# mLSTM denominators summed on GpSimd with one product by ones per head, and position-bias tiles laid out by the host

## The chip, the cores and the metric

The kernel runs on one core of one Trainium2 chip. The metric is the device time of one execution in microseconds (us), lower is better. The engines are TensorE (PE, with its weight loads shown as PEld), VectorE (DVE), ScalarE (ACT), GpSimd (POOL) and SyncE (SP, which here only issues DMAs). Each engine works through its own queue in order.

## What is computed

One decoder layer on a sequence of 512 tokens and 1024 features: RMSNorm, one wide projection, two parallel token mixers (an mLSTM with 4 heads of 128, and differential attention with 4 heads), a gated merge, a gated convolutional FFN, a per-layer embedding and a final norm. The parts that the change touches are these lines, cut from the reference:

```python
# mLSTM, a head: weights of keys for queries, numerator and denominator
sqk = jnp.einsum('bhcld,bhcsd->bhcls', qc, kc) * dmat
num = (...
       + jnp.einsum('bhcls,bhcse->bhcle', sqk, vc))
den = s_inter * ... + jnp.sum(sqk, -1)
h = num / jnp.maximum(jnp.abs(den), jnp.exp(-m_t))[..., None]
# differential attention: scores of a half of a head
bucket = t5_causal_bucket(q_pos, k_pos)
bias = jnp.moveaxis(rel_bias[bucket], -1, 0)
...
s = jnp.einsum('bhqd,bhkd->bhqk', qb, kk, ...) * scale + bias
```

The kernel evaluates the mLSTM not in chunks of 64 but over the whole sequence at once, which is the same sum; so `den` of a head is the column sum, over all 512 keys, of a matrix of weights that is zero where the key comes after the query.

## The kernel before, in words

Activations lie with features on the 128 partitions and the 512 tokens along the free dimension. Every product is made of three passes (`mm3`, lines 96 to 99): each operand is split into a high part and a low part (`split`, line 87: a copy on ACT, a subtraction on DVE), and high x high, high x low and low x high are accumulated in PSUM. Weights come in chunks of 128 x 1024 (`wload`, line 101), each loaded by SP, cast by ACT (L89) and completed by DVE (L90), with two buffers each for `raw`, `whi` and `wlo`.

The program is a Python trace; a planner then orders each engine's queue when the program is built, by program order as priority and by its own estimates of time, and hands out buffers by tag. Nothing is reordered on the chip. The string `ORDER` gives the order of the steps of both branches: `bias0` and `if0` (gates) come first, then projections `mq`, `mk` with convolution, the cores `m0` to `m3` of the mLSTM heads and their ends `M0` to `M3`, then attention (`dq`, `dk`, `dv`, cores `a`, ends `A`), with the merge gates `ga`, `gb` as work in between.

A core `m` (function `mlstm`) runs over four blocks of 128 keys, j = 0 to 3. For each it loads a row of gate terms to all partitions (`rb`, SP, L419; widths 512, 384, 256, 128), takes the exponential (ACT, L420), clears the upper triangle of the diagonal block (POOL, L421), multiplies by the scores `s` from PSUM (DVE, L425) and splits the result into `ph` and `pl`. `weighted` (L381) then multiplies them by V into `num` (three passes) and by a matrix of ones into `den` (two passes, L394 and L395). The PSUM widths are 512, 384, 256 and 256 columns; the last block is padded with zeros by POOL. `den` has every row equal to the column sum. The tag `rb` has three buffers, `hn` four, the PSUM tag `acc` two.

`mlstm_end` reads `den` (L442), forms a correction for the norm and normalises `num`; its norm uses `colsum` (L157): copy on ACT (L159), subtraction on DVE (L160), two products with ones (L161, L162).

`gates` (`if0`) makes the gate pre-activations from one projection, and runs a chain of small DVE and ACT operations: products (L302, L303), sums (L306), logarithm of the sigmoid (L309 to L313), a running maximum (L317), four running sums (L322). The columns that ACT needs as biases are transposed on PE into `colp` (L331).

`make_bias` (`bias0`) makes the attention's Toeplitz tiles on the chip: a table, two one-hot matrices by DMA, two full-precision products on PE (`bvp`, L347), a copy scaled by 8 on ACT, a row in DRAM, a broadcast of it to 128 rows in DRAM, and four skewed loads of 256 KB from there, all of these DMAs on POOL's queue. `make_nlam` loads the lambda vectors and reduces them on DVE. In `attention` a DVE instruction (L467) adds scores and bias with the scale 0.125 and takes the maximum.

Of the kernel before, what the change touches and what calls it, by code (L numbers as in the profile page):

```python
# [20 lines left out]
H = 4  # L21
# [11 lines left out]
# columns of the packed per-feature parameters  # L33
# [8 lines left out]
# offsets of a head's broadcast gate rows: one run for each block of keys, then -m  # L42
# [3 lines left out]
# chunks that ScalarE scales for the final norm; the last ones are scaled as they are normed  # L46
NSCALED = 6

# the steps of the two branches, by priority: projections, then the cores (m, a) and their ends (M, A)
ORDER = """  # L50
bias0 if0 mq0 mk0 mq1 mk1 m0 m1 mk3 mq2 dk0 M0 M1 mk2 m2 mq3 M2 m3 dq0 dv0 M3 a0 dk1 dq1
# [5 lines left out]
def trunk_kernel(ctx, tc, xT, pT, par, oneh, relb, lamv, w_if, w_in, w_v, w_br, w_out, w_up,  # L57
# [88 lines left out]
    def rsqrt_of(r, v, a, before=None):  # L146
        """r = v ** -0.5: from its logarithm, then one Newton step; a is scratch."""
# [44 lines left out]
    def win(c):  # L192
        return wload(w_in[c])

    def conv_silu(c, scale, name):
# [3 lines left out]
        nc.gpsimd.memset(u[:, 0:3], 0.0)  # L199
# [13 lines left out]
    def halves(c, name):  # L213
        """a head's two halves of 64 features, each in its own rows."""
        o = ps("mm", name)
        proj(o, win(c), 0, h)
        y = tt("ev", "y")
        nc.vector.tensor_mul(y, o, rB)
        return y, (slice(0, 64), slice(64, P))

    def queries(c, name):
        """for each half, one operand with its two parts above one another."""
        y, rows = halves(c, name)
# [8 lines left out]
    def keys(c, name):  # L232
        """for each half, its first part twice, and its second part beside zeros."""
# [12 lines left out]
    def vw(i, g, kk, old):  # L246
        """a half at a time, so that the first products can start early."""
# [42 lines left out]
    def gates():  # L290
        # few columns: the second parts of the weights stand beside the first ones
# [45 lines left out]
    def make_bias():  # L337
        tab = cp.tile([REL_BUCKETS + 1, H], F32, name="tab")
        nc.vector.memset(tab, NEG)
        nc.gpsimd.dma_start(tab[0:REL_BUCKETS, :], relb)  # L340
        bvd = dp.tile([H, 640], F32, name="bvd")
        for i in range(2):
            half = slice(i * 320, (i + 1) * 320)
            oh = tt("hn", "oh", 320)[0:REL_BUCKETS + 1, :]
            nc.gpsimd.dma_start(oh, oneh[:, half])
            o = ps("acc", "bvp", 320)
            nc.tensor.matmul(o[0:H, :], lhsT=tab, rhs=oh, start=True, stop=True)  # L347
            bv = tt("hn", "bv", 320)[0:H, :]
            nc.scalar.activation(bv, o[0:H, :], AF.Copy, scale=8.0)
            nc.gpsimd.dma_start(bvd[:, half], bv)  # L350
        rows = dp.tile([P, H * 640], F32, name="bvrows")
        nc.gpsimd.dma_start(rows, bvd.rearrange("h u -> (h u)").partition_broadcast(P))
        bias = []
        for hh in range(H):
            t = f(rt("bt", f"bias{hh}"))
            src = bass.AP(tensor=rows.tensor, offset=rows[0, hh * 640 + P - 1:hh * 640 + P].offset,
                          ap=[[H * 640 - 1, P], [1, S]])
            nc.gpsimd.dma_start(t, src)
            bias.append(t)
        return bias  # L360
# [17 lines left out]
    def wide(j):  # L378
        """columns of a block of keys: of all the later queries, 256 at the least."""
        return min(j * P, S - 2 * P)  # L380

    def weighted(name, j, src_parts, v, hh, outs):
        """products with V (and with ones) of one block of keys; src_parts fills the block's pair."""
# [6 lines left out]
        o = outs[0][:, wide(j):]  # L390
        mm3(o, [t[:, hh * P:(hh + 1) * P] for t in v[j]], (ph, pl), j == 0, j == NB - 1)
        if len(outs) > 1:
            o = outs[1][:, wide(j):]
            nc.tensor.matmul(o, lhsT=ones, rhs=ph, start=j == 0, stop=False)  # L394
            nc.tensor.matmul(o, lhsT=ones, rhs=pl, start=False, stop=j == NB - 1)  # L395

    def head_norm(o, g, name, extra=None):
        """y = o * g * rsqrt(mean square of o over a head's 128 features + extra)."""
# [15 lines left out]
    def mlstm(hh):  # L414
        num, den = ps("acc", f"num{hh}"), ps("acc", f"den{hh}")
        for j in range(NB):
# [9 lines left out]
            weighted("p", j, lambda a, b: split(a, b, rb), mv, hh, (num, den))  # L426
# [27 lines left out]
    def attention(hh, q, k):  # L454
        av = []
        for i in range(NB):
# [3 lines left out]
            for z in range(2):  # L460
                s = ps("sc", f"ds{hh}{i}{z}", nw)
                for b in range(2):
# [5 lines left out]
                    out=e, in0=s[:, :n], in1=bias[hh][:, S - n:], scale=0.125, scalar=-3.0e38,  # L468
# [10 lines left out]
        for j in range(NB):  # L479
# [3 lines left out]
            weighted("a", j, lambda a, b: split(a, b, tps), dv, hh, (o,))  # L483
# [213 lines left out]
def _fmajor(a):  # L697
    """(S, K*128) -> (128, K, S)."""
    return a.T.reshape(a.shape[1] // P, P, a.shape[0]).transpose(1, 0, 2)
# [70 lines left out]
```

## Time and profile before

| what | value |
|---|---|
| three runs | 835.82, 835.96, 836.72 us (median 835.96) |
| profiled execution: span from first to last instruction | 833.1 us |
| median less that span | 2.9 us |
| PE busy | 809.5 us of the span (97%) |
| DVE, ACT, POOL busy | 552.0, 423.5, 25.0 us |
| mean granted TensorE clock, as a share of full speed | 0.991 |

The profile gives one execution's span and no separate time for what lies around it; the runs' median is 2.9 us above it. Matmul durations in the trace overlap, since matmuls are pipelined; what one costs the engine is read from the start of one to the start of the next. "Idle before" is the time for which the engine had nothing running ahead of an instruction, with what ended it.

### The profile page before, as it was taken

To read this page: it belongs to the slowest core of one execution; us is meant where nothing else is said; L and a number is where in the kernel's file an instruction comes from. 1 tells how busy PE (TensorE), PEld (TensorE's weight loads), DVE (VectorE), ACT (ScalarE), POOL (GpSimd) and SP (SyncE) were. 2 spreads that over 40 slices of the span, in tenths; PEclk is the share of its full clock that TensorE was granted. 3 is DMA by queue.
4 is the path that set the end of the run, shared out by engine and by line. 5 is a ranking of instruction groups with operands and counts; after the bars stand their busy time and mean duration, and the time that the engine had idled before them with its cause. 6 is when DMAs were issued, how large, how long until landed. Compare 5 with 4: busy or idle time off the path is not lost.

```text
span 833.1 us, 9821 instructions
## 1 busy us (share of the span) xinstructions
PE 809.5 (97%) x3626; PEld 662.6 (80%) x3626; DVE 552.0 (66%) x877; ACT 423.5 (51%) x627; POOL 25.0 (3%) x110
## 2 busy tenths in 40 slices
PE   6999999999999999999999999999999999999993
PEld 5778788887878888888788888888888888888883
DVE  6588888699767854456677777777777333343676
ACT  6546887687776433234654444444445332222653
POOL 0111100000000000000000000000000000000000
PEclk9999999999999999999999999999999999999997
DMA  6263323221222223352333322223322333333212
GB/s 222 92 207 111 116 97 123 89 77 62 66 76 76 76 102 101 122 182 95 107 102 101 101 95 87 98 101 101 101 89 89 94 96 111 90 95 95 100 53 101
DMA packets 29143, 85.42 MB, mean 103 GB/s; under 512 B 3286, under 2 KB 7018, under 8 KB 28968
## 3 DMA queue, kind: packets, MB, share of 16 engines
q1 hardware_dynamic: 28424, 82.22, 30.5%
q0 software_dynamic: 672, 2.59, 1.0%
q8 instruction: 28, 0.46, 0.2%
q14 instruction: 19, 0.16, 0.1%
HBM read 82.66 MB, written 3.45 MB: 103 GB/s over the span
## 4 chain that ended last, share of the span: by engine, by line
PE 90%; DVE 3%; ACT 2%; DMA 2%; issue 1%; SPq 0%; DVEq 0%; ACTq 0%
PE wd L99 5%; PE uv L97 5%; PE wd L97 5%; PE uv L99 5%; PE uv L98 5%; PE wd L98 5%; PE ug L97 5%; PE ug L99 5%; PE ug L98 5%; PE ga L97 2%; PE ga L99 2%; PE ga L98 2%; PE wo L97 2%; PE gb L97 2%; PE gb L98 2%; PE gb L99 2%
## 5 line engine op out<-in xcount | busy, mean ns | idle before, releaser
L89 ACT CAST whi<-raw 128x1024 fp32r<-128x1024 f32 (+1 forms) x143 | 144.5, 1012 | 214.3 <-PE wd L98 71.2
L90 DVE TENSOR_TENSOR wlo<-raw,whi 128x1024 fp32r<-128x1024 f32 (+1 forms) x142 | 167.1, 1178 | 90.0 <-ACT whi L89 88.7
L97 PE MATMUL wd<-gh,whi 128*128 128x512 f32 x176 | 68.5, 389 | 0.0
L98 PE MATMUL wd<-gl,whi 128*128 128x512 f32 x176 | 68.5, 389 | 0.0
L99 PE MATMUL wd<-gh,wlo 128*128 128x512 f32 x176 | 68.5, 389 | 0.0
L576 DVE SCALAR_TENSOR_TENSOR y<-u,prm,y 128x512 f32<-128x512 f32 x88 | 65.6, 748 | 1.5
L89 ACT CAST gh<-y 128x512 fp32r<-128x512 f32 x22 | 13.7, 621 | 55.5 <-DVE y L585 55.5
L571 DVE TENSOR_TENSOR u<-uv,rffn 128x512 f32<-128x512 f32 x22 | 15.2, 692 | 38.1 <-PE uv L99 38.1
L98 PEld LDWEIGHTS wd<-gl,whi 128*128 128x128 f32 x176 | 33.0, 188 | 6.9
L99 PEld LDWEIGHTS wd<-gh,wlo 128*128 128x128 f32 x176 | 33.0, 188 | 6.9
L97 PEld LDWEIGHTS wd<-gh,whi 128*128 128x128 f32 x176 | 33.0, 188 | 6.8
L574 ACT ACTIVATE y<-u,prm 128x512 f32<-128x512 f32 x44 | 35.7, 814 | 0.5 <-DVE u L571 0.3
L583 ACT ACTIVATE y<-y 128x512 f32<-128x512 f32 x22 | 13.9, 632 | 40.6 <-DVE y L576 40.6
L90 DVE TENSOR_TENSOR gl<-y,gh 128x512 fp32r<-128x512 f32 x22 | 15.2, 692 | 14.7 <-ACT gh L89 14.7
L97 PE MATMUL wo<-mxh,whi 128*128 128x512 f32 x64 | 24.9, 389 | 0.0
L98 PE MATMUL wo<-mxl,whi 128*128 128x512 f32 x64 | 24.9, 389 | 0.0
L99 PE MATMUL wo<-mxh,wlo 128*128 128x512 f32 x64 | 24.9, 389 | 0.0
L143 ACT ACTIVATE sq<-x 128x512 f32<-128x512 f32 x27 | 16.7, 620 | 9.3 <-DVE x L633 9.3
L471 ACT ACTIVATE e<-e,mx 128x128 f32<-128x128 f32 (+3 forms) x32 | 17.8, 558 | 7.0 <-DVE mx L470 6.8
L144 DVE TENSOR_TENSOR acc<-acc,sq 128x512 f32<-128x512 f32 x27 | 18.5, 686 | 3.1 <-ACT sq L143 3.0
L205 DVE SCALAR_TENSOR_TENSOR y<-u,prm,y 128x512 f32<-128x512 f32 x24 | 17.9, 745 | 2.0 <-ACT y L203 1.9
L559 DVE TENSOR_TENSOR x<-x,wo 128x512 f32<-128x512 f32 x8 | 5.5, 688 | 17.1 <-PE wo L99 17.1
(1060 smaller groups left out, 2206.1 us busy)
## 6 DMA issues: line engine op xcount, KB each, us to landing
raw<-in_w_up SPq DMA_DIRECT2D x44, 512.0 KB, 3.2
raw<-in_w_in SPq DMA_DIRECT2D x36, 512.0 KB, 3.3
raw<-in_w_down SPq DMA_DIRECT2D x16, 512.0 KB, 3.5
x<-in_xT SPq DMA_DIRECT2D x16, 256.0 KB, 4.4
raw<-in_w_br SPq DMA_DIRECT2D x8, 512.0 KB, 3.2
raw<-in_w_out SPq DMA_DIRECT2D x8, 512.0 KB, 3.7
raw<-in_w_gate SPq DMA_DIRECT2D x8, 512.0 KB, 3.2
raw<-in_w_down SPq DMA_DIRECT2D x8, 384.0 KB, 3.1
```

The costliest lines, as they stand in the source:

```text
L89: nc.scalar.copy(hi, src)
L90: nc.vector.tensor_sub(lo, src, f(hi))
L97: nc.tensor.matmul(o, lhsT=lh, rhs=rh, start=start, stop=False)
L98: nc.tensor.matmul(o, lhsT=lh, rhs=rl, start=False, stop=False)
L99: nc.tensor.matmul(o, lhsT=ll, rhs=rh, start=False, stop=stop)
L143: nc.scalar.activation(q, src, AF.Square)
L144: nc.vector.tensor_add(acc, acc, q)
L205: nc.vector.scalar_tensor_tensor(y, u[:, i:i + S], col(c0 + i), y, op0=ALU.mult, op1=ALU.add)
L471: nc.scalar.activation(e, e, AF.Exp, bias=mx[:, 1:2], accum_out=mx[:, 2:3])
L571: nc.vector.tensor_mul(u[:, 2:514], o, rB)
L574: nc.scalar.activation(y, u[:, 2:514], AF.Identity, scale=col(c0 + 2), bias=col(c0 + 3))
L576: nc.vector.scalar_tensor_tensor(y, u[:, i:i + S], col(c0 + i), y, op0=ALU.mult, op1=ALU.add)
```

## The change

Four things change.

1. `weighted` no longer multiplies the blocks by ones. Instead `mlstm` keeps the tile `rb` of block 0 as `total`, adds the tiles of blocks 1 to 3 to its columns on GpSimd, and makes one `colsum` of it into `den`.
2. `make_bias` only loads four finished tiles of 256 KB from an input `biasT`, which the host lays out (`_bias_tiles`). The step `bias0` moves from the front of `ORDER` to behind `mk2`; the loads, still on POOL's queue, are issued after the last small memset that POOL did for a convolution. `make_nlam` moves with the step.
3. The scale 1/8 moves from the attention's DVE instruction (its `scale` is now 1.0) to the queries' scaling by the norm, which becomes a `scalar_tensor_tensor` instead of a `tensor_mul`; the factor 8 on the bias goes.
4. Comments and docstrings go; they change nothing.

```diff
-bias0 if0 mq0 mk0 mq1 mk1 m0 m1 mk3 mq2 dk0 M0 M1 mk2 m2 mq3 M2 m3 dq0 dv0 M3 a0 dk1 dq1
+if0 mq0 mk0 mq1 mk1 m0 m1 mk3 mq2 dk0 M0 M1 mk2 bias0 m2 mq3 M2 m3 dq0 dv0 M3 a0 dk1 dq1
...
-        nc.gpsimd.memset(u[:, 0:3], 0.0)
+        nonlocal last_pool
+        last_pool = nc.gpsimd.memset(u[:, 0:3], 0.0)
...
-    def halves(c, name):
+    def halves(c, name, scale=1.0):
...
-        nc.vector.tensor_mul(y, o, rB)
+        nc.vector.scalar_tensor_tensor(y, o, scale, rB, op0=ALU.mult, op1=ALU.mult)
...
     def make_bias():
-        tab = cp.tile([REL_BUCKETS + 1, H], F32, name="tab")
...
-            nc.tensor.matmul(o[0:H, :], lhsT=tab, rhs=oh, start=True, stop=True)
...
+        out = []
         for hh in range(H):
             t = f(rt("bt", f"bias{hh}"))
-            src = bass.AP(tensor=rows.tensor, offset=rows[0, hh * 640 + P - 1:hh * 640 + P].offset,
-                          ap=[[H * 640 - 1, P], [1, S]])
-            nc.gpsimd.dma_start(t, src)
-            bias.append(t)
-        return bias
+            with tc.issue_after(last_pool.ins):
+                nc.gpsimd.dma_start(t, biasT[:, hh * S:(hh + 1) * S])
+            out.append(t)
+        return out
...
-    def weighted(name, j, src_parts, v, hh, outs):
+    def weighted(name, j, src_parts, v, hh, o):
...
-        o = outs[0][:, wide(j):]
-        mm3(o, [t[:, hh * P:(hh + 1) * P] for t in v[j]], (ph, pl), j == 0, j == NB - 1)
-        if len(outs) > 1:
-            o = outs[1][:, wide(j):]
-            nc.tensor.matmul(o, lhsT=ones, rhs=ph, start=j == 0, stop=False)
-            nc.tensor.matmul(o, lhsT=ones, rhs=pl, start=False, stop=j == NB - 1)
+        mm3(o[:, wide(j):], [t[:, hh * P:(hh + 1) * P] for t in v[j]], (ph, pl), j == 0, j == NB - 1)
...
-            weighted("p", j, lambda a, b: split(a, b, rb), mv, hh, (num, den))
+            weighted("p", j, lambda a, b: split(a, b, rb), mv, hh, num)
+            if j == 0:
+                total = rb
+            else:
+                nc.gpsimd.tensor_add(total[:, j * P:], total[:, j * P:], rb)
+        colsum(den, total)
         return num, den
...
-                    out=e, in0=s[:, :n], in1=bias[hh][:, S - n:], scale=0.125, scalar=-3.0e38,
+                    out=e, in0=s[:, :n], in1=bias[hh][:, S - n:], scale=1.0, scalar=-3.0e38,
```

## Rows read from the trace of the kernel before

**Rows 1.** The page, part 1: busy us (share of the span) xinstructions.
```profile
PE 809.5 (97%) x3626; PEld 662.6 (80%) x3626; DVE 552.0 (66%) x877; ACT 423.5 (51%) x627; POOL 25.0 (3%) x110
```

**Rows 2.** Windows by stage, the mLSTM's: length, busy us (xinstructions), PEclk, DMA share, GB/s.
```profile
65.00:155.00 90.00, 88.95 (x421) 73.37 (x421) 74.13 (x116) 69.93 (x113) 9.17 (x31) 1.00 0.32 106
```

**Rows 3.** Waits of PE: what waited for whom: us in total, times, longest.
```profile
PE colp L331 <- DVE cols L323: 1.6, 1, 1.6
PE num L97 <- ACT pph L89: 1.0, 3, 0.4
```

**Rows 4.** Timeline of PE, head 1: start us, us, line, out<-in, shape.
```profile
87.75 0.39 PE L99 MATMUL num<-pph,mvl 128*128 128x512 f32 x1
87.98 0.40 PE L395 MATMUL den<-ppl,ones 128*128 128x512 f32 x1
...
88.74 0.33 PE L394 MATMUL den<-pph,ones 128*128 128x384 f32 x1
88.92 0.33 PE L395 MATMUL den<-ppl,ones 128*128 128x384 f32 x1
89.09 0.28 PE L97 MATMUL num<-pph,mvh 128*128 128x256 f32 x1
89.21 0.28 PE L394 MATMUL den<-pph,ones 128*128 128x256 f32 x1
```

**Rows 5.** Timeline of PE around the first product of the position bias.
```profile
32.77 0.39 PE L99 MATMUL mvp<-whi,h7l 128*128 128x512 f32 x1
...
33.09 0.70 PE L347 MATMUL bvp<-oh,tab 33*4 33x320 f32 x2
...
33.72 0.50 PE L300 MATMUL if<-h0h,whi 128*128 128x512 f32 x1
```

**Rows 6.** Timeline of PE around a column sum of today's head norm.
```profile
109.38 0.50 PE L161 MATMUL hm1ss<-csph,ones 128*128 128x512 f32 x1
...
109.72 0.39 PE L98 MATMUL mk<-h7l,whi 128*128 128x512 f32 x1
...
110.18 0.42 PE L162 MATMUL hm1ss<-cspl,ones 128*128 128x512 f32 x1
...
110.44 0.40 PE L97 MATMUL mq<-h0h,whi 128*128 128x512 f32 x1
```

**Rows 7.** Groups of ACT and of DVE, 60 to 160 us: xcount, busy us, mean ns.
```profile
L159 ACT CAST csph<-v 128x512 fp32r<-128x512 f32 x4 | 2.5, 620 | 0.1
...
L160 DVE TENSOR_TENSOR cspl<-v,csph 128x512 fp32r<-128x512 f32 x4 | 2.8, 690 | 1.7 <-ACT csph L159 1.7
```

**Rows 8.** Groups of POOL: xcount, busy us, mean ns, idle before.
```profile
L421 POOL TENSOR_SCALAR_AFFINE_SELECT rb<-rb 128x128 f32<-128x128 f32 x16 | 5.8, 361 | 48.7 <-ACT rb L420 40.7 <-DVE ppl L90 5.7 <-issue 2.4
```

**Rows 9.** Timeline of DVE and POOL side by side, from 81.65 us.
```profile
81.65 1.23 DVE L90 TENSOR_TENSOR wlo<-raw,whi 128x1024 fp32r<-128x1024 f32 x1 [0.24 <-ACT whi L89]
...
82.77 0.85 POOL L421 TENSOR_SCALAR_AFFINE_SELECT rb<-rb 128x128 f32<-128x128 f32 x1 [2.39 <-issue]
82.79 0.69 DVE L93 SCALAR_TENSOR_TENSOR mk1l<-y,mk1h 128x512 fp32r<-128x512 f32 x1
```

**Rows 10.** Timeline of PE around its wait for the gate columns.
```profile
50.34 0.39 PE L99 MATMUL mq<-h1h,wlo 128*128 128x512 f32 x1
...
52.31 0.22 PE L331 MATMUL colp<-ident,cols 4*128 4x4 f32 x1 [1.58 <-DVE cols L323]
...
57.03 0.39 PE L99 MATMUL mq<-h5h,wlo 128*128 128x512 f32 x1
```

**Rows 11.** Window behind that wait, columns as in rows 2.
```profile
52.40:57.00 4.60, 4.60 (x13) 3.49 (x14) 4.60 (x11) 0.63 (x1) 0.00 (x0) 0.63 0.60 212
```

**Rows 12.** Timeline of DVE, start of the gate chain.
```profile
37.68 0.68 DVE L302 TENSOR_TENSOR gt<-if,rmix 36x512 f32<-36x512 f32 x1 [1.52 <-PE if L300]
...
40.21 0.69 DVE L303 TENSOR_TENSOR g<-if,rmix 36x512 f32<-36x512 f32 x1
```

**Rows 13.** Waits of SP's own queue, columns as in rows 3.
```profile
SPq L419 <- DVE ppl L90: 17.8, 8, 4.0
```

More of the change, by code (lines that the diff above doesn't have):

```diff
@@ L56, in trunk_kernel @@
 @with_exitstack
-def trunk_kernel(ctx, tc, xT, pT, par, oneh, relb, lamv, w_if, w_in, w_v, w_br, w_out, w_up,
+def trunk_kernel(ctx, tc, xT, pT, par, biasT, lamv, w_if, w_in, w_v, w_br, w_out, w_up,
                  w_down, w_gate, w_ple, out):
@@ L193, in win @@
         return wload(w_in[c])
+    last_pool = None
     def conv_silu(c, scale, name):
@@ L217, in halves @@
         y = tt("ev", "y")
-        nc.vector.tensor_mul(y, o, rB)
+        nc.vector.scalar_tensor_tensor(y, o, scale, rB, op0=ALU.mult, op1=ALU.mult)
         return y, (slice(0, 64), slice(64, P))
     def queries(c, name):
-        y, rows = halves(c, name)
+        y, rows = halves(c, name, 0.125)
         qs = []
@@ L337, in make_bias @@
     def make_bias():
-        tab = cp.tile([REL_BUCKETS + 1, H], F32, name="tab")
[L339 to L346, printed above, removed]
-            nc.tensor.matmul(o[0:H, :], lhsT=tab, rhs=oh, start=True, stop=True)
[L348 to L353, printed above, removed]
+        out = []
         for hh in range(H):
             t = f(rt("bt", f"bias{hh}"))
-            src = bass.AP(tensor=rows.tensor, offset=rows[0, hh * 640 + P - 1:hh * 640 + P].offset,
-                          ap=[[H * 640 - 1, P], [1, S]])
-            nc.gpsimd.dma_start(t, src)
-            bias.append(t)
-        return bias
+            with tc.issue_after(last_pool.ins):
+                nc.gpsimd.dma_start(t, biasT[:, hh * S:(hh + 1) * S])
+            out.append(t)
+        return out
     def make_nlam():
@@ L482, in attention @@
                 nc.tensor.transpose(tps[:, (i - j) * P:(i - j + 1) * P], av[i][:, j * P:(j + 1) * P], ident)
-            weighted("a", j, lambda a, b: split(a, b, tps), dv, hh, (o,))
+            weighted("a", j, lambda a, b: split(a, b, tps), dv, hh, o)
         return o
@@ L703, in _cols, with _bias_tiles @@
     return v.reshape(-1, P).T
-def _bucket_onehot():
-    u = np.arange(640)
-    n = np.maximum(511 - u, 0)
+def _bias_tiles(rel_bias):
+    n = P * (NB - 1) + np.arange(P)[:, None] - np.arange(S)[None, :]
+    future = n < 0
+    n = np.maximum(n, 0)
     exact = REL_BUCKETS // 2
@@ L713, in _bucket_onehot @@
     b = np.where(n < exact, n, np.minimum(large, REL_BUCKETS - 1))
-    b = np.where(u <= 511, b, REL_BUCKETS)
-    return (b[None, :] == np.arange(REL_BUCKETS + 1)[:, None]).astype(np.float32)
+    t = np.concatenate([rel_bias, np.full((1, H), NEG, np.float32)])[np.where(future, REL_BUCKETS, b)]
+    return t.transpose(0, 2, 1).reshape(P, H * S)
 def _pack(x, p, rel_bias, norm_mix_g, w_in, b_if, m_conv_w, m_conv_b, m_norm_g, da_lambda, da_norm_g,
@@ L743, in _pack @@
     return {
-        "xT": _fmajor(x[0]), "pT": _fmajor(p[0, 0]), "par": par, "oneh": _bucket_onehot(),
-        "relb": rel_bias, "lamv": da_lambda[0],
+        "xT": _fmajor(x[0]), "pT": _fmajor(p[0, 0]), "par": par, "biasT": _bias_tiles(rel_bias), "lamv": da_lambda[0],
         "w_if": gif.reshape(KD, P, 64).transpose(1, 0, 2).reshape(P, KD * 64), "w_in": _chunks(win), "w_v": wv,
```

## The prediction

> **What bounds the kernel now.** I read the busy times of the engines first. TensorE is busy for 809.5 of 833.1 us, 97%; VectorE, the next, for 66% [rows 1]. A busy share is only an average, so the second view is the stage that the change touches, from 65 to 155 us, where the four mLSTM heads run between projections: TensorE is busy for 88.95 of 90 us there at a granted clock of 1.00, VectorE for 74.1, ScalarE for 69.9, GpSimd for 9.2 [rows 2]. VectorE has thus 15.9 us to spare in that stage, GpSimd 80. The third view is what TensorE waits for: in this part of the program one wait of 1.6 us for the gate columns (`colp`), and three of 1.0 us together for the split weights of a block (`num`) [rows 3]. So while one head's chain runs over ScalarE, VectorE and GpSimd, TensorE works on the next projections. What leaves TensorE's queue shortens the run; what is added elsewhere is free as long as it doesn't hold TensorE up. The weights, gates and merge after it keep TensorE supplied with products that need none of this, so a head that ends a few us later is no loss by itself.
>
> **The change part by part.** Costs on TensorE are distances from one start to the next, since the durations overlap.
>
> *The products with ones* go: for each head and each of the two split parts, one of 512 columns, one of 384 and two of 256. The distances are 0.23 us (87.75 to 87.98), 0.175 (88.74 to 88.92 to 89.09) and 0.12 (89.09 to 89.21) [rows 4]; a part costs 0.23 + 0.175 + 2 x 0.12 = 0.645 us, and 4 x 2 x 0.645 = 5.2 us go. They lie among other matmuls without a gap, so all of it is on the path.
>
> *The new column sum* of each head is two products of 512 columns, which wait for ScalarE's copy and VectorE's subtraction. Today's column sum of a norm shows the price: 109.38 to 109.72 and 110.18 to 110.44, 0.34 + 0.26 = 0.60 us [rows 6]; without any trouble at the wait it would be 2 x 0.23 = 0.46 [rows 4]. I take 0.60: 4 x 0.60 = 2.4 us come back (bound below: 1.8).
>
> *The two bias products* (`bvp`) go. From the matmul ahead of the first to the one behind it are 33.72 - 32.77 = 0.95 us where 0.23 would be usual [rows 4, 5]: 0.72 each, and 1.4 us for the two (the second, at 37.57, has the same distances around it).
>
> *The rest of the column sum*: four copies of 0.62 us on ScalarE and four subtractions of 0.69 us on VectorE [rows 7], 2.5 and 2.8 us. ScalarE's 20 and VectorE's 15.9 us of idle time in the stage hide them [rows 2]. Without that cover the whole 2.8 us would be lost.
>
> *The additions on GpSimd*: three a head, of 384, 256 and 128 columns, twelve in all. The trace of before has no operation with two inputs on GpSimd. The nearest row is the selection over 128 columns with one input, 0.361 us [rows 8]. If its time doesn't grow with the columns, a head's additions take 3 x 0.361 = 1.1 us; if it grows with the columns, 768/128 x 0.361 = 2.2 us; if a second input doubles that, 4.3 us. I take 2.2, by the nearest row, 8.7 us in all on an engine that is idle for 80 us of this stage. An addition needs the product of line 425 alone, so it runs beside the split of the same block, and only the last one, the smallest, stands before the column sum. Can it also cost VectorE something? A selection that started at 82.77 beside a weight subtraction of two inputs took 0.85 us instead of 0.36 [rows 8, 9], so one of the two engines was held by the other. If every us of the additions held VectorE up, it would lose 8.7 + 2.8 = 11.5 us in this stage, less than its 15.9 idle; this can't reach TensorE in the sum, only at single places (rivals).
>
> The Trainium skill speaks against this part: "GPSIMD Engine Reference", section 3.1, advises VectorE for elementwise work and has an addition of 2,048 fp32 columns at 4,497 ns on GpSimd and 2,293 ns on VectorE; by that a head's additions would be an estimated 1.7 us, and the sum here would stay as it is, for GpSimd isn't what ends last. Of the holding-up it states the rule ("SBUF — State Buffer", section "Who interferes with whom"): a VectorE instruction with two SBUF inputs and a GpSimd one that reads SBUF exclude each other, and the second waits. The 0.85 us above agree with it. Were VectorE the bound of the stage, up to 6.7 us would be lost by that estimate.
>
> *Buffers*: `total` now holds one of the three `rb` buffers until its column sum has been split. SP's loads of `rb` waited already for such a buffer, eight times, 17.8 us in all, behind VectorE's split [rows 13]. What is queued behind them on SP are weight loads. With two buffers the next head's first load comes about one block later. The planner knows of that and puts other loads first; I cost it at nothing, and at the "new waits" rival below if it doesn't fit.
>
> *The bias tiles and lambda*: the table, one-hot loads, row, broadcast and the skewed loads leave the front of POOL's queue; four plain loads of 256 KB go into it behind `mk2`'s memset, with heads 2 and 3 of the mLSTM still between them and the attention that reads them. They stand ahead of the selections of head 2 on POOL, as four instructions that only issue. Off the path, 0; were attention to come to them early, it would wait for a load. `make_nlam`'s small VectorE operations leave the gate chain: the second gate product starts 2.5 us after the first, at 40.21 instead of behind 38.36 [rows 12]; in between lie a weight subtraction and a lambda product. The new queries' instruction replaces one on the same tile; four in all, off the path.
>
> **The sum.** 5.2 + 1.4 - 2.4 = 4.2 us less on TensorE. The profiled span of 833.1 us becomes 828.9. The three runs' median is 835.96, 2.9 us above that span; nothing in the change lies outside the span, so I keep the 2.9: 831.8 us.
>
> **The rivals.**
>
> *The gate wait goes too.* TensorE stands from its last matmul's start at 50.34 to 52.31, 1.74 us more than a matmul needs [rows 10], and the granted clock then has a mean of 0.63 over 4.6 us, that is, partly the lower level, 1.2 GHz [rows 11], which loses another 4.6 x 0.37 = 1.7. The wait ends with VectorE's gate chain, and that gets shorter by the lambda work and by the 2.5 us above [rows 12]. For it: the chain really loses work. Against it: the planner sees the shorter chain as well and puts `colp` earlier into TensorE's queue; the wait is where its estimate of the chain was too short, and that may stay as it is. If all goes: 831.8 - 3.4 = 828.4 us.
>
> *New small waits eat the gain.* The column sums stand in TensorE's queue at a place that the planner chose by its estimates. Eight new products wait, four for ScalarE and four for VectorE. If each costs what the longest wait of `num` costs, 0.4 us [rows 3], with 0.1 for the restart (0.34 instead of 0.23 in rows 6), that is 8 x 0.5 = 4.0: 835.8 us.
>
> *The late column sum, slower.* The chain of block 3 is product, addition on GpSimd, copy on ScalarE, products; the addition is new in it. GpSimd works in order, and it can be held by VectorE [rows 9] or be behind a bias load. ScalarE then stands at the copy, with a weight cast queued behind it, and TensorE stands at the column sum with every later product behind. If that happens in two heads at the price of the gate wait with its clock, 2 x 3.4 = 6.8 us against the 4.2: 838.6 us. The change becomes slower than before from 4.2 us of new waits on, measurably so from about 5.9. Against it speaks that today's similar chain over GpSimd's selection costs three waits of 0.4 us at most [rows 3].
>
> **How the numbers follow.** Chances: the sum with the gate wait as it is, 831.8 us, 0.42 (its own range 830.0 to 833.5, from the bounds of the column sum and a wait more or less); the gate wait gone, 828.4 us, 0.28; small waits, 835.8 us, 0.15; the late column sum, 838.6 us, 0.15. A difference of 0.2%, 1.7 us, is about what a measurement of this kernel can tell from no change: faster means below 834.3, slower above 837.6. The first two cases are faster, 0.70; the third is the same, 0.15; the fourth slower, 0.15. For the range I leave out the fourth case and the tails: from 828.4 less 0.6 (column sums at their lower bound) and 0.6 (some of the `num` waits), 827.2, to the third case and one us more, 836.8.
>
> **What the profile after would show.** Right, if TensorE has 28 matmul records fewer (32 products with ones and two records of each bias product [rows 5], against eight new ones), if the column sums of `den` cost 0.5 to 0.6 us each from start to start with no gap ahead of them, if GpSimd's busy time rises by some 9 us without TensorE naming `den` among its waits, and if VectorE's share in the mLSTM stage rises while TensorE's stays near 99%. The `colp` row decides between the first two cases: its wait and the clock behind it. The forecast is wrong if TensorE waits for `csph` or `cspl` of `den` for more than a us in a head, if ScalarE or VectorE stand behind GpSimd with weight casts queued, if SP's `rb` waits grow until a projection waits for its weights, or if the planner's new order opens gaps somewhere else, in attention above all, where GpSimd has hardly any part.

## The result and the profile after

The changed kernel takes 849.14 us (median of four runs, 848.54 to 849.73), the kernel before 836.34 us on the same chip (835.82 to 836.84): the ratio is 1.0158, 95% interval [1.0146, 1.0170]. The change makes the kernel 13 us slower; 831.8 us were forecast, with 836.8 as the upper end. Every set of runs below had the kernel before run beside it (medians of 834.95 to 836.34 us); the ratios are to those runs and aren't always exactly the quotients of the medians.

The profiled execution after has a span of 847.4 us, 14.3 more than before. The first part of its page, busy time of each engine, share of the span, instructions:

```profile
span 847.4 us, 9766 instructions
...
PE 811.6 (96%) x3598; PEld 659.1 (78%) x3598; DVE 560.6 (66%) x880; ACT 431.8 (51%) x635; POOL 35.1 (4%) x116
```

Beside [rows 1] TensorE has 28 matmul records fewer, as forecast, and yet is busy longer; GpSimd, 25.0 us busy before, has 10.1 us more. The records of matmuls beside a wait are longer (0.79 us for the one at 127.99, behind the longest wait, where 0.39 is usual), so busy time alone doesn't tell, and the next view is what TensorE waits for (us in total, times, longest):

```profile
PE s L97 <- ACT mk2h L92: 5.8, 1, 5.8
PE num L98 <- DVE ppl L90: 2.1, 4, 0.8
PE yb L97 <- ACT hdh L92: 2.0, 1, 2.0
...
PE colp L334 <- DVE cols L326: 1.6, 1, 1.6
PE mo L99 <- DVE wlo L90: 1.0, 1, 1.0
```

Of these only `colp` stood in [rows 3] at this length. New are one wait of 5.8 us for the keys of head 2 (`mk2h`, from ScalarE), four of 2.1 us together for the second part of a block's weights (`ppl`, from VectorE; the longest wait for split weights before was 0.4), and one of 2.0 us for the end of an attention head (`hdh`). `den`, on which the forecast's slower rival rested, isn't among them. The busy time of the engines in stretches of the span (length, then PE, PEld, DVE, ACT, POOL with instructions, the granted clock, the DMA share, GB/s):

```profile
95.00:130.00 35.00, 27.38 (x114) 21.04 (x113) 25.46 (x40) 34.29 (x48) 5.88 (x14) 0.93 0.35 108
122.00:128.00 6.00, 0.15 (x2) 0.01 (x1) 2.14 (x4) 5.96 (x9) 0.28 (x1) 0.75 0.14 36
128.00:132.00 4.00, 4.00 (x10) 3.13 (x11) 4.00 (x10) 4.00 (x7) 0.31 (x1) 0.52 0.01 4
```

And one stretch of the kernel before, in the same columns:

```profile
95.00:130.00 35.00, 35.00 (x159) 28.55 (x157) 29.62 (x44) 27.62 (x42) 2.36 (x7) 1.00 0.31 102
```

Between 95 and 130 us TensorE was busy all the time before; after, it has 27.4 of 35 us, and it is ScalarE that is full: 34.3 us instead of 27.6. From 122 to 128 TensorE does next to nothing, and behind that the granted clock is 0.52, that is, nearly all of four us at the lower level, 1.2 GHz. In this stretch lie the norms of mLSTM heads 0 and 1, their output gates, the convolutions of head 2 and the weight casts of the next projections. ScalarE's timeline there (start, duration, line, operation):

```profile
100.00 1.28 ACT L150 ACT_TABLE_LOAD   x1
101.28 1.28 ACT L421 ACT_TABLE_LOAD   x1
102.58 0.63 ACT L421 ACTIVATE mo<-mo 128x512 f32<-128x512 f32 x1
...
105.74 1.28 ACT L151 ACT_TABLE_LOAD   x1
107.04 0.63 ACT L151 ACTIVATE r<-v 128x512 f32<-128x512 f32 x1
...
110.11 1.28 ACT L152 ACT_TABLE_LOAD   x1
111.41 0.72 ACT L152 ACTIVATE r<-r,lnb 128x512 f32<-128x512 f32 x1
...
121.92 1.28 ACT L151 ACT_TABLE_LOAD   x1
123.21 0.63 ACT L151 ACTIVATE r<-v 128x512 f32<-128x512 f32 x1
123.86 1.28 ACT L210 ACT_TABLE_LOAD   x1
125.15 0.63 ACT L210 ACTIVATE u<-y 128x512 f32<-128x512 f32 x1
125.69 0.71 ACT L152 ACTIVATE r<-r,lnb 128x512 f32<-128x512 f32 x1
...
127.33 0.61 ACT L92 ACTIVATE mk2h<-y 128x512 fp32r<-128x512 f32 x1
127.85 1.03 ACT L89 CAST whi<-raw 128x1024 fp32r<-128x1024 f32 x1
```

The lines with a load are the key. Line 150 preloads the table that holds logarithm and exponential, so that lines 151 (logarithm) and 152 (exponential) need none. Here the tangent of an output gate (line 421, at 102.58) has come between: it loads its own table at 101.28, the logarithm loads one at 105.74 and the exponential another at 110.11. One norm takes four loads of 1.28 us in place of the preload and one for the next tangent. In the kernel before, the norm of head 0 has its logarithm right from the preload:

```profile
94.47 1.28 ACT L150 ACT_TABLE_LOAD   x1
...
96.92 0.62 ACT L151 ACTIVATE r<-v 128x512 f32<-128x512 f32 x1
...
98.03 1.28 ACT L207 ACT_TABLE_LOAD   x1
...
101.33 0.71 ACT L152 ACTIVATE r<-r,lnb 128x512 f32<-128x512 f32 x1
```

There a tangent stands between logarithm and exponential, and the exponential at 101.33 needs no load behind the tangent's. So it is the tangent ahead of the logarithm that costs two loads more. The same happens in the norm of head 1 behind it, and in attention's last norm at 282 us, from where the wait for `hdh` comes. `mk2h`, for which TensorE stands until 127.99, is the instruction at 127.33, behind all that. The trace has 29 loads after and 23 before, in this stretch 8 and 3 (a fourth of before, the one at 94.47, lies just ahead of it). But for the preloads none of them stands in the kernel's text; they are put in when the program is built.

The last view of after is GpSimd's, by groups (busy us, mean ns of one):

```profile
L403 POOL TENSOR_SCALAR_AFFINE_SELECT rb<-rb 128x128 f32<-128x128 f32 x16 | 6.9, 433 | 63.4 <-ACT rb L402 63.0 <-DMA raw<-in_w_in 0.4
L412 POOL TENSOR_TENSOR rb<-rb 128x256 f32<-128x256 f32 x4 | 5.0, 1251 | 0.2
L412 POOL TENSOR_TENSOR rb<-rb 128x384 f32<-128x384 f32 x4 | 4.9, 1214 | 13.4 <-DVE ppl L90 8.4 <-DVE rb L407 5.0
...
L412 POOL TENSOR_TENSOR rb<-rb 128x128 f32<-128x128 f32 x4 | 2.5, 634 | 2.0 <-DVE rb L407 2.0
```

The additions (line 412) take 12.4 us, 1.21, 1.25 and 0.63 us for 384, 256 and 128 columns. How they and VectorE hold one another shows at 134.68, first GpSimd, then VectorE:

```profile
134.68 1.02 POOL L412 TENSOR_TENSOR rb<-rb 128x384 f32<-128x384 f32 x1 [5.02 <-DVE rb L407]
...
135.78 1.59 POOL L412 TENSOR_TENSOR rb<-rb 128x256 f32<-128x256 f32 x1
```

```profile
134.78 2.00 DVE L90 TENSOR_TENSOR wlo<-raw,whi 128x1024 fp32r<-128x1024 f32 x1
136.71 1.08 DVE L90 TENSOR_TENSOR ppl<-rb,pph 128x384 fp32r<-128x384 f32 x1
```

A weight subtraction of 1,024 columns started while an addition ran and took 2.00 us; the mean of all such is 1.24. The second addition started beside it and took 1.59; the block's subtraction started beside that and took 1.08 where 0.55 is usual with nothing beside it. In all, ten VectorE instructions of after are longer than their kind in this way, by 4.9 us together; before, none.

### The profile page after: what moved, and what is told of

Same layout as the page of the kernel before. It is cut to its first block, busy times and chain, and to the rows that moved or that the text cites. A ratio compares the mean times of both kernels' runs of the same rounds, so it can differ in the third digit from the quotient of the medians.

```text
span 847.4 us, 9766 instructions
## 1 busy us (share of the span) xinstructions
PE 811.6 (96%) x3598; PEld 659.1 (78%) x3598; DVE 560.6 (66%) x880; ACT 431.8 (51%) x635; POOL 35.1 (4%) x116
## 4 chain that ended last, share of the span: by engine, by line
PE 82%; ACT 7%; DVE 7%; issue 2%; DMA 1%; POOL 0%; SPq 0%; DVEq 0%; ACTq 0%
PE wd L99 5%; PE wd L97 5%; PE uv L97 5%; PE uv L98 5%; PE uv L99 5%; PE wd L98 5%; PE ug L97 5%; PE ug L98 5%; PE ug L99 5%; PE gb L99 2%; PE gb L98 2%; PE gb L97 2%; PE ga L97 2%; PE ga L99 2%; PE ga L98 2%
## 5 line engine op out<-in xcount | busy, mean ns | idle before, releaser
L90 DVE TENSOR_TENSOR gl<-y,gh 128x512 fp32r<-128x512 f32 x22 | 15.2, 692 | 14.6 <-ACT gh L89 14.6
L557 POOL MEMSET u<- 128x2 f32 x44 | 4.3, 100 | 371.3 <-DVE y L563 361.3
```

The costliest lines, as they stand in the source:

```text
L90: nc.vector.tensor_sub(lo, src, f(hi))
```

## The experiments

Two suspicions, then: the table loads that fell into the norms, and the additions on GpSimd beside VectorE. The rival to both is the order itself: the planner has laid all instructions out anew, and the loads may only have come along. All runs in one table; loads are those in the trace, in brackets the ones between 95 and 130 us; the last two columns are the busy us of ScalarE and TensorE in those 35 us, from the view of stretches.

| kernel | loads | us | ratio to before [95%] | ScalarE | TensorE |
|---|---|---|---|---|---|
| before | 23 (3) | 836.34 | 1 | 27.6 | 35.0 |
| after | 29 (8) | 849.14 | 1.0158 [1.0146, 1.0170] | 34.3 | 27.4 |
| adds_dve | 29 (8) | 841.59 | 1.0071 [1.0053, 1.0090] | 33.0 | 28.9 |
| before_no_tanh | 15 (1) | 835.56 | 1.0000 [0.9990, 1.0009] | 26.7 | 34.6 |
| after_no_tanh | 15 (2) | 835.94 | 0.9999 [0.9990, 1.0008] | 28.4 | 33.3 |
| adds_dve_no_tanh | 15 (2) | 832.89 | 0.9967 [0.9955, 0.9979] | 28.3 | 34.4 |
| idle_adds | 23 (4) | 838.63 | 1.0039 [1.0024, 1.0054] | 29.4 | 34.7 |
| bias_only | 25 (5) | 837.82 | 1.0021 [1.0011, 1.0030] | 30.2 | 33.0 |
| den_only | 27 (8) | 843.81 | 1.0100 [1.0083, 1.0117] | 33.2 | 28.7 |
| before_loads | 30 (8) | 842.40 | 1.0083 [1.0064, 1.0101] | 32.7 | 31.9 |
| dve_no_tanh_loads | 21 (8) | 841.40 | 1.0078 [1.0062, 1.0094] | 32.9 | 28.2 |
| after_grouped | 25 (6) | 845.48 | 1.0109 [1.0085, 1.0134] | 32.9 | 29.3 |
| after_sorted | 23 (4) | 839.48 | 1.0052 [1.0035, 1.0068] | 31.5 | 33.0 |
| dve_sorted | 23 (4) | 839.15 | 1.0042 [1.0027, 1.0057] | 28.7 | 32.5 |
| dve_m0_early | 25 (4) | 839.24 | 1.0045 [1.0032, 1.0057] | 29.1 | 31.3 |
| dve_m0_first | 25 (3) | 841.05 | 1.0066 [1.0054, 1.0078] | 28.5 | 31.0 |
| before_exp | 5 (0) | 836.14 | 1.0014 [1.0005, 1.0023] | 31.5 | 33.8 |
| after_exp | 5 (0) | 837.18 | 1.0017 [1.0006, 1.0027] | 31.1 | 32.2 |
| dve_exp | 5 (0) | 838.93 | 1.0044 [1.0030, 1.0057] | 30.2 | 29.4 |
| bias_exp | 5 (0) | 842.08 | 1.0082 [1.0069, 1.0096] | 29.8 | 30.1 |

**Additions and tangents, each alone and both.** adds_dve moves the additions to VectorE. The `no_tanh` kernels replace the tangents of convolution, output gate and merge gate by the identity, at which no trace here has a load: these three nonlinearities are left out in them.

```diff
-                nc.gpsimd.tensor_add(total[:, j * P:], total[:, j * P:], rb)
+                nc.vector.tensor_add(total[:, j * P:], total[:, j * P:], rb)
```
```diff
-        nc.scalar.activation(t, y, AF.Tanh, scale=0.5)
+        nc.scalar.activation(t, y, AF.Identity, scale=0.5)
```

> The changed kernel with the twelve additions on VectorE instead of GpSimd. Rival L (GpSimd and VectorE hold each other up): the stretched VectorE instructions, 4.9 us in all, go, and the time falls to 832 to 838 us. Theory T (function tables): ScalarE's queue still loads tables three times within the ends M0 and M1, so TensorE still waits several us for mk2; 845 to 851 us.

> The kernel before with the tangents of the convolutions, output gates and merge gates replaced by a scaled copy (Identity), which needs no table of its own; the gates' and convolutions' nonlinearity is left out, all else is as before. It is the partner of after_no_tanh. Theory T: eight table loads fewer on ScalarE, which is not the bound before: 832 to 836 us.

> The changed kernel with the same tangents replaced by a scaled copy; that nonlinearity is left out, all else is as in the change. No table switch is left inside the mixers but the norms' own. Theory T: 0 to 5 us below before_no_tanh, since TensorE's 4.2 us are saved and the waits for mk2 and hd3 are gone. Rival L: the additions still hold VectorE, so 8 us or more above before_no_tanh.

> The changed kernel with the additions on VectorE and without the tangents of the mixers (a scaled copy instead; that nonlinearity is left out): neither of the two suspected causes is left. If the tables and GpSimd's additions each cost their own, the 7.5 us between the change and adds_dve come off after_no_tanh's 835.9: 828 us, and TensorE's saved 4.2 us show. If GpSimd's additions matter only where ScalarE's queue is full of table loads, it stays at 834 to 836 us.

Measured: 841.59, 835.56, 835.94 and 832.89 us. Without the tangents the kernel before is as fast as with them, and the changed kernel loses its whole 13 us. With the additions on VectorE as well, it is 2.7 us faster than before_no_tanh: that much of the forecast's 4.2 us appears here. The additions on GpSimd cost 3.0 us where the tangents are out (835.94 - 832.89; 2.7 by the ratios) and 7.5 where they are in (849.14 - 841.59; 7.3 by the ratios). adds_dve lies between the ranges expected by either theory, so neither cause alone is the loss; after_no_tanh ends 0.4 us above its partner where 0 to 5 us below were expected, and adds_dve_no_tanh between its two cases. One stretch of adds_dve_no_tanh, in the columns from above:

```profile
95.00:130.00 35.00, 34.39 (x154) 27.23 (x153) 31.86 (x52) 28.28 (x45) 5.49 (x15) 1.00 0.41 133
```

ScalarE has 28.3 us there, TensorE 34.4: no longer full, and TensorE is supplied. That speaks for the tables, but the tangents also bind the order, so it isn't proof yet.

**The additions alone.** idle_adds is the kernel before with twelve additions on GpSimd of the same sizes, whose result nobody reads:

```diff
...
+            if j:
+                nc.gpsimd.tensor_add(dum[:, j * P:], rb, rb)
```

> The kernel before with twelve additions on GpSimd of 384, 256 and 128 columns, beside the splits of the mLSTM blocks, whose results nobody reads (each block's tile added to itself into a spare tile); the products with ones stay. ScalarE's queue has as many table loads as before, 23. Rival L (the holding-up by itself costs the time): VectorE instructions stretched by about 5 us in all, and the time 4 to 8 us above before. Theory T together with the idle time of VectorE: stretched as well, but hidden; 0 to 2 us above before.

Measured: 838.63 us, 1.0039 [1.0024, 1.0054], some 3 us, as in the pair above, and between the two ranges that were expected. Nobody reads these additions; they can act through VectorE, the buffers, what stands behind them in GpSimd's queue, and the order, which hardly moved (591 of ScalarE's some 600 instructions in the trace keep theirs). Their groups:

```profile
L430 POOL TENSOR_TENSOR dum<-rb 128x384 f32<-128x384 f32 x4 | 4.5, 1137 | 13.9 <-issue 8.5 <-DVE rb L425 5.4
...
L430 POOL TENSOR_TENSOR dum<-rb 128x256 f32<-128x256 f32 x4 | 3.5, 878 | 6.8 <-DVE rb L425 6.8
L430 POOL TENSOR_TENSOR dum<-rb 128x128 f32<-128x128 f32 x4 | 2.9, 724 | 2.7 <-DVE rb L425 2.7
```

That is 10.9 us on an engine with 80 us to spare, and 3 us reach the end. Eight VectorE instructions are stretched, by 3.3 us together. Where this meets TensorE shows in the waits of its weight loads for VectorE's part of a block's weights. Before has none; here, and in after:

```profile
PEld num L98 <- DVE ppl L90: 3.3, 8, 0.7
```

```profile
PEld num L98 <- DVE ppl L90: 4.8, 6, 1.2
```

With the additions on VectorE they are 0.9 us (adds_dve) and 0.2 (adds_dve_no_tanh). A wait of 0.9 us for `mk0h` in idle_adds, at 68.58, comes ahead of the first addition (72.45) and isn't theirs.

**The two parts.** bias_only makes the bias part alone (tiles from the host, step `bias0` moved, scaled queries), den_only the denominators alone.

> The kernel before with the second part of the change alone: bias tiles from the host, the step moved behind mk2, the scale moved to the queries; the products with ones stay. TensorE does 1.4 us less; ScalarE's queue has 25 table loads, with the pattern of three extra loads in M1 alone. By the sum of the prediction 834.3 to 834.6 us. Theory T: one such end costs some 2 to 4 us of waiting, 835 to 839 us.

> The kernel before with the first part of the change alone: weights added up on GpSimd, one column sum, with the bias made on the chip as before. ScalarE's queue has 27 table loads, with the pattern in M0 and M1 but not in A3. By the sum of the prediction 833 us. Theory T with rival L: the wait for mk2 and the small waits for split weights stay, that for hd3 goes: 843 to 850 us.

Measured: 837.82 and 843.81 us, 2.2 and 8.2 us more than before; both together cost 13. In den_only the stretch is as in after (8 loads, ScalarE 33.2). In bias_only one tangent falls into the norm of head 1. So the bias part wasn't free either.

**The loads alone.** before_loads adds one instruction to the norms of heads 0 and 1: a tangent of one column that nobody reads, between preload and logarithm. dve_no_tanh_loads does the same to adds_dve_no_tanh (with its nonlinearities left out). The rest nearly keeps its order: of ScalarE's some 600 instructions in the traces, the loads left out, 573 keep it in the first and 586 in the second (from before to after it is 529).

```diff
+        if extra:
+            tiny = tp.tile([P, 4], F32, tag="mx", name="tiny", bufs=8)
+            nc.scalar.activation(tiny[:, 0:1], v[:, 0:1], AF.Tanh, scale=0.5)
         nc.scalar.activation(r, v, AF.Ln, scale=2.0 ** -LN_SHIFT)
```

> Kernel before, with one more instruction in the norms of mLSTM heads 0 and 1: a tangent of one column that nobody reads, between the preload and the logarithm, so that tangent, logarithm and exponential each need a table: 30 loads in the program in place of 23, and the order of the other instructions on ScalarE nearly that of the kernel before. Nothing of the change is in it. Theory (such loads, in a stretch where ScalarE has some 5 us to spare, are what costs the time): 6 to 8 loads of 1.28 us more between 95 and 130 us, ScalarE without idle time there, TensorE late by 4 to 9 us, so 840 to 845 us. Rival (the new order of the planner costs it, the loads lie in idle time): below 837.5 us.

> adds_dve_no_tanh (832.9 us, with the change's saving on TensorE in it, three nonlinearities left out) with the same tangent of one column in the norms of heads 0 and 1: 21 loads in place of 15. Theory: ScalarE has 30.8 of 35 us between 95 and 130 us there and gets 7.7 us more, so it is full and TensorE is late by 4 to 8 us: 837 to 841 us. Rival: below 834.5 us.

Measured: 842.40 us (1.0083 [1.0064, 1.0101]) and 841.40, that is 7.4 and 8.5 us more than the kernels that they come from (6.9 and 9.3 by the ratios), for seven and six loads more. The first is the kernel before with nothing of the change in it, and its ScalarE timeline shows what stood in after:

```profile
95.35 1.28 ACT L150 ACT_TABLE_LOAD   x1
...
97.91 1.28 ACT L153 ACT_TABLE_LOAD   x1
99.21 0.20 ACT L153 ACTIVATE tiny<-v 128x1 f32<-128x1 f32 x1
...
100.89 1.28 ACT L154 ACT_TABLE_LOAD   x1
102.18 0.63 ACT L154 ACTIVATE r<-v 128x512 f32<-128x512 f32 x1
...
103.35 1.28 ACT L155 ACT_TABLE_LOAD   x1
104.65 0.72 ACT L155 ACTIVATE r<-r,lnb 128x512 f32<-128x512 f32 x1
...
124.90 0.61 ACT L92 ACTIVATE mk2h<-y 128x512 fp32r<-128x512 f32 x1
```

```profile
PE s L97 <- ACT mk2h L92: 1.7, 1, 1.7
```

In dve_no_tanh_loads it is the weight cast of the next projection that comes late:

```profile
PE dq L97 <- ACT whi L89: 3.9, 1, 3.9
```

Loads inside norms are thus enough for 7 to 9 us, in the range expected of the loads or just above it, and far from the rival's. In dve_no_tanh_loads all six are in the norms of heads 0 and 1. In before_loads four are; the other three fell into the norm of head 2 (141.77 to 147.89), where the layout put a tangent behind the preload too. In that run TensorE's nth matmul is 0.9 us later than in before at 99 us, 5.6 at 131 and 7.5 at 162: some two thirds of the loss arise beside the first two norms.

**Putting the loads elsewhere.** after_grouped lets each tangent come behind the last norm's exponential; after_sorted and dve_sorted (additions on VectorE) also let the preload come behind the last tangent written before it. dve_m0_early and dve_m0_first move one step in the list instead, with the additions on VectorE.

```diff
+        with tc.issue_after(last_exp.ins):
+            last_tanh = nc.scalar.activation(t, src, AF.Tanh, scale=0.5)
...
-            with tc.issue_after(before.ins):
+            with tc.issue_after(before.ins), tc.issue_after((last_tanh or before).ins):
                 nc.scalar.preload_act_table_set("natural_log_exp_and_others")
```
```diff
-if0 mq0 mk0 mq1 mk1 m0 m1 mk3 mq2 dk0 M0 M1 mk2 bias0 ...
+if0 mq0 mk0 mq1 mk1 m0 m1 mk3 M0 mq2 dk0 M1 mk2 bias0 ...    (dve_m0_early)
+if0 mq0 mk0 mq1 mk1 m0 M0 m1 mk3 mq2 dk0 M1 mk2 bias0 ...    (dve_m0_first)
```

> The changed kernel; every hyperbolic tangent of the convolutions, output gates and merge gates is queued on ScalarE behind the exponential of the norm traced before it, so that none stands between a norm's logarithm and exponential. Theory T (function tables): the loss comes from table loads that the new order of ScalarE's queue needs, 3 of 1.28 us beyond the usual two in each of the ends M0, M1 and A3, which make mk2 and hd3 late and TensorE wait 6.0 and 2.2 us. With the tangents out of the way the waits go: 831 to 837 us, no wait of TensorE over 2 us in the mLSTM and none for hd3. Rival L (GpSimd holds VectorE): the twelve additions are still there, so 845 us or more.

> The changed kernel with the function tables sorted from both sides: a norm's table load is queued on ScalarE behind the last tangent traced before it, and each tangent behind the exponential of the norm traced before it. 23 table loads as in the kernel before, none between a norm's logarithm and exponential; the twelve additions stay on GpSimd. Theory T: the table loads are most of the loss; 836 to 840 us, with the some 3 us that GpSimd's additions cost without them (after_no_tanh against adds_dve_no_tanh). If the loss is not the number of loads but that both ends M0 and M1 crowd ScalarE at 100 to 130 us, it stays above 842 us with ScalarE over 9.3 of 10 busy there.

> As after_sorted, with the additions on VectorE: both suspected causes are away and nothing is left out. Theory T with L: near adds_dve_no_tanh, 832 to 836 us, faster than the kernel before if the sorting itself costs no waits. If crowding is the cause, 838 to 842 us.

> Changed kernel, complete, additions on VectorE, and in the list of steps M0 (the end of mLSTM head 0) two places earlier, behind mk3: the planner then lays the norm of head 0 out so that no tangent falls between its preload and its exponential; 25 loads in the program in place of 29, and none inside the norms of heads 0 and 1 (one pair inside a norm of attention). Theory (loads in the full stretch of ScalarE): TensorE loses less than 3 us between 95 and 130 us, so 832 to 836 us, against 841.6 of adds_dve. Rival (the order around heads 0 and 1 costs it, whatever the loads do): 838 us or more.

> The same with M0 right behind m0, ahead of head 1's core; 25 loads too, none inside the norms of heads 0 and 1, which also lie further apart (the preload of head 0 some 15 ScalarE instructions earlier). Theory: 831 to 835 us. Rival: 838 us or more.

Measured: 845.48, 839.48, 839.15, 839.24 and 841.05 us. after_grouped missed: it only keeps tangents from standing between logarithm and exponential, and loads still fell into the norm of head 0. (A norm hit in this way has two loads beyond the usual two, as counted above, not the three of that expectation.) after_sorted gives back 8.9 us of the loss (1.0158 to 1.0052), with no load between preload and exponential; dve_sorted, dve_m0_early and dve_m0_first missed, 839 to 841 us where 831 to 836 were expected, and landed where their rivals (crowding, or the order whatever the loads do) had put them. There no tangent stands between preload and logarithm in these two norms (3 or 4 loads in the stretch), ScalarE has 28.5 to 29.1 us of the 35, and TensorE still only 31 to 32.6. The loads aren't all of it: against adds_dve (841.59), taking them out of the norms gave 2.4 us back at the most.

**No tangents and all of the work.** The `exp` kernels work the three sigmoids out with exponential and logarithm, which need no load between them here, and drop the preloads that this makes idle. That costs two more operations of 0.62 us on ScalarE for each sigmoid (written out here; in the kernel the three stand in a helper).

```diff
-        nc.scalar.activation(t, y, AF.Tanh, scale=0.5)
-        nc.vector.scalar_tensor_tensor(y, t, 1.0, y, op0=ALU.add, op1=ALU.mult)
+        nc.scalar.activation(t, y, AF.Exp, scale=-1.0)
+        nc.scalar.activation(t, t, AF.Ln, bias=1.0)
+        nc.scalar.activation(t, t, AF.Exp, scale=-1.0)
+        nc.vector.scalar_tensor_tensor(y, t, 2.0, y, op0=ALU.mult, op1=ALU.mult)
```

> Kernel before, with the sigmoids of convolution, output gate and merge gates worked out as Exp, Ln (bias 1), Exp on ScalarE in place of one Tanh, and without the preloads that this makes idle: 4 table loads in the program in place of 23, at the price of two more ScalarE operations of some 0.62 us for each sigmoid. All of the computation is there. In the kernel before the loads cost nothing (before_no_tanh, 835.56 against 835.68 us), so by either theory this is 834 to 838 us; above 838 would mean that the added ScalarE operations themselves reach TensorE, and then only the differences among these four kernels say anything.

> Changed kernel with the same sigmoids, complete. Theory (table loads between a norm's preload, logarithm and exponential are what cost 13.2 us): within 2 us of before_exp, 834 to 839 us, no wait of TensorE for a ScalarE operation over 2 us, and some 4 to 5 us of stretched VectorE operations left. Rival (the planner's new order around the heads costs it, whatever the tables do, and leaving the nonlinearity out had only made the chains shorter): 843 us or more, with a long wait for mk2h as before.

> Changed kernel with the same sigmoids and with the additions on VectorE, complete. Theory: GpSimd's additions cost 3 us beside VectorE also here, so 831 to 834 us, 2 to 4 us below before_exp and after_exp: the forecast's saving on TensorE then shows. Rival (additions on VectorE were better only since they changed the order): no more than 1 us from after_exp.

> Bias part alone on the kernel before, with the same sigmoids, complete. Theory (its 2.2 us alone came of one pair of table loads inside a norm and of waits of 1.4 to 1.6 us behind them): 1 to 2 us below before_exp, the two bias products that it saves. Rival (four plain loads of 256 KB in POOL's queue or the new query instruction cost it): 1.5 to 3 us above before_exp.

Measured: ratios of 1.0014, 1.0017, 1.0044 and 1.0082 (the trace has five loads in each, none of them in the stage). after_exp and before_exp differ by 0.0003 with intervals of 0.001, as the tables' theory wanted: with the loads gone from both, the change costs nothing. By itself that proves little, since the other two missed it, and their rivals too: dve_exp is slower than after_exp, and bias_exp is 6 us slower than before_exp with as few loads. Its ScalarE timeline shows how that goes without a load:

```profile
103.50 1.03 ACT L89 CAST whi<-raw 128x1024 fp32r<-128x1024 f32 x1
...
114.94 1.04 ACT L89 CAST whi<-raw 128x1024 fp32r<-128x1024 f32 x1
...
120.32 1.03 ACT L89 CAST whi<-raw 128x1024 fp32r<-128x1024 f32 x1
...
123.94 1.05 ACT L89 CAST whi<-raw 128x1024 fp32r<-128x1024 f32 x1 [2.18 <-DVE y L213]
```

```profile
PE mo L97 <- ACT whi L89: 1.9, 1, 1.9
...
PE dq L99 <- DVE wlo L90: 1.9, 1, 1.9
```

Two weight casts (line 89, `whi`) are 11.4 us apart, with norms, gates, sigmoids and the casts of `dk0` in ScalarE's queue between them; the projections that use them (`mo`, `dq`) wait. So ScalarE can hold TensorE up here by its order alone. What made the planner choose this order in bias_exp, dve_exp and the two kernels with M0 moved, and not in before_exp, no run tells apart; that stays open.

## Why the prediction was wrong

*What bounds the stage.* [Rows 2] were read as 70 us of ScalarE in 90, some 20 spare. In the 35 us where the heads' ends meet the next projections it was 27.6 of 35, and TensorE depended on ScalarE's order there. A mean over 90 us hid the stretch with the least room.

*The products with ones, the column sums, the bias products.* Right. 28 records fewer; the column sums of `den` cost 0.47, 0.57, 0.67 and 0.68 us from start to start (83.24 to 83.47 and 84.18 to 84.42 for the first), 2.4 us in all as costed, and no matmul waits for `den`. By these distances TensorE has 4.2 us less to do. adds_dve_no_tanh brings 2.7 of them to the end of the program; where ScalarE or VectorE is late instead, they turn into waiting.

*"ScalarE's 20 and VectorE's 15.9 us of idle time in the stage hide them."* This is the step that failed. The four copies as such (2.5 us) would have fitted. But the step took ScalarE's instructions as the only work there. Six more table loads, 7.7 us, came with the new order, four of them into the norms of heads 0 and 1 and two into attention's last; no part of the forecast counted them, though 23 stood in the trace of before. What such loads cost shows in before_loads and dve_no_tanh_loads, 7 to 9 us. The rest of this step's failure is the order itself: with the loads out of these norms TensorE still has only 31 to 32.6 of the 35 us (dve_sorted and the two with M0 moved).

*The additions on GpSimd: 2.2 us a head, off the path.* Undersized, and the wrong conclusion. They take 12.4 us in place of 8.7, 3.1 a head, inside the bounds of 1.1 and 4.3 that were given. That they hold VectorE up was said, with 8.7 us at the most (11.5 with the column sums' subtractions); measured are 4.9. "This can't reach TensorE in the sum, only at single places" was where it went wrong: the single places are the split weights of the blocks, where TensorE stands behind VectorE (`num`, 2.1 us for matmuls, 4.8 for weight loads), and they cost some 3 us in two pairs of runs that agree. In dve_exp against after_exp these waits go too (4.1 us of weight loads in after_exp, none in dve_exp), but waits for weight casts come in their place (`dq` 2.1, `dvp` 1.7) and the time is longer, so the 3 us don't hold in any order. The Trainium skill, "SBUF — State Buffer", section "Who interferes with whom", has the two engines lock each other out of the port pair that they share, and the order of issue decide which one waits; the 2.00 and 1.59 us at 134.78 and 135.78 agree. By the addition of 2,048 columns in 4,497 ns that the Trainium skill has ("GPSIMD Engine Reference", section 3.1) 384 columns would be an estimated 0.84 us; the trace has 1.21 beside a busy VectorE.

*The bias tiles and lambda: off the path, 0.* Wrong alone: 2.2 us (bias_only) in place of 1.4 saved. The step moved `bias0` in the list, and the order behind it changed; what of it costs the time stays open (bias_exp).

*Buffers: nothing.* Nothing speaks against it: SP's loads of `rb` wait 14.6 us behind VectorE's split, 17.8 before, and 2.1 us more for the column sum's split and an addition.

*The rivals.* The gate wait stayed at 1.6 us (`colp`), as the likeliest case had it. The 2.5 us that its rival counted on are from start to start; between the end of the first gate product (38.36) and the second (40.21) lie 1.85. The small waits came as foreseen in kind, for `num`, but for VectorE's split, not for the column sums. The late column sum named the right engine and the right consequence, ScalarE standing with others' casts behind it, and the wrong reason: what filled ScalarE were loads and the order of its own work, not a wait for GpSimd. "Its new order opens gaps somewhere else" was named at the end, without a price and without a chance.

*How the 17.3 us between forecast and result divide* isn't settled to the last: the 3.0 us of the additions and the 7 to 9 of such loads are each shown alone, the loads in kernels that lack the change or its nonlinearities; with tangents in and additions on GpSimd together the two cost more than their sum (the additions 7.5 instead of 3), and the order holds a part that shows in dve_m0_early (839.24, with no tangent between preload and logarithm in the two norms).

## What to carry to other kernels

Look for the stretch in which a helper engine is nearly full, and take its slack from there, not from the stage; count table loads as work of ScalarE, and see whether an edit can push one function between another's preload and its use. A list of steps doesn't show the loads, so look for them in the trace. An idle engine that shares a resource with a busy one isn't free room: price the busy engine's delay first, with an addition that nobody reads.

None of the kernels here that do all of the work is faster than the kernel before.

## What the runs showed of the chip that was not expected

- A logarithm and an exponential that follow it take two table loads where a tangent has come between preload and logarithm: 105.74 and 110.11 in after, 100.89 and 103.35 in before_loads. The Trainium skill, "ScalarE: Activation LUTs", section "Table sets: the hidden batching unit", counts one load for that pair, since one table has both; that agrees in these traces only where no tangent stands between the preload and the logarithm. The same page of the Trainium skill, section "What ACT_TABLE_LOAD costs", has 1,283 ns for the load, as every one here, and a drain of some 1,380 ns besides; in these rows the next load or operation starts 1.28 to 1.30 us after a load does, and the load at 123.86 starts 0.02 us after the logarithm ahead of it ends, so no such drain is seen.
- GpSimd additions of 256 columns took as long as those of 384 (means of 1.25 and 1.21 us) beside a busy VectorE.
- Twelve additions that nobody reads and that lay on an idle engine cost some 3 us of 836 (idle_adds).
